# Rates of the conditioning tiles in the first layer: 0.9 a chunk in the query stage, 0.5 in the output projection

## The chip, the cores and the metric

The kernel runs on one core of a Trainium2 chip. The metric is the device time of one execution in microseconds (us), median of the runs. The profile is of one further execution of the same program.

## What is computed

The reference is a trunk of two decoder layers over 256 tokens of 2048 features. Layer 0 mixes tokens by an indexer that keeps 64 keys per query, layer 1 by block attention; a SwiGLU network follows each. Every sub-layer is wrapped in norms and modulated by a conditioning vector c:

```
c_act = silu(c)
for i in range(2):
    mod = c_act @ ada_w[i] + ada_b[i]            # 6 parts of 2048 numbers
    sh1, sc1, g1, sh2, sc2, g2 = split(mod, 6)
    h = rms_norm(x, norm_g[i, 0]) * (1 + sc1) + sh1
    y = (dsa_mixer if i % 2 == 0 else moba_mixer)(h, ...)      # projections, attention, y = o @ w_o
    x = x + g1 * rms_norm(y, norm_g[i, 1])
    h = rms_norm(x, norm_g[i, 2]) * (1 + sc2) + sh2
    x = x + g2 * rms_norm(swiglu(h, ...), norm_g[i, 3])
```

All is in float32. The weights `ada_w` are 2 x 2048 x 12288 numbers, of which each is used once: they are a matrix-vector product that has only to be streamed.

## The kernel before, in words

A weight matrix is read in chunks of 128 partitions x 1024 numbers (512 KB): `load_split` (line 247) issues the load into a `raw` buffer (5 of them), then ScalarE (ACT) copies it to `hi`, a rounded float32r part, and VectorE (DVE) writes the rest, `lo = raw - hi` (line 245; 4 buffers each). TensorE (PE) multiplies by both. All loads are issued by SyncE (SP, "SPq" in the profile), one after the other in program order: an issue that must wait for its buffer holds all later ones up.

The conditioning weights come as tiles of 128 x 2048 (1 MB) into the two `ada` buffers. A column tile (`ada_tile`, line 148) is multiplied with c on VectorE (line 151). A row tile (`ada_row_tile`, line 163) is multiplied on TensorE (line 171); after the 16th, ScalarE copies the sum out (line 176). A buffer is free for the next tile once its product is done.

When a tile is issued is set by a table of rates. `pace` fills a queue of tiles and sets `Pace.rate`; after each chunk load `tick` (line 202) adds the rate to `Pace.due` and issues one tile for each whole number reached. Here the queue holds 48 tiles: parts 4 and 3 of layer 0 (32 column tiles), mixed with 16 row tiles. `Pace.due` starts at 5.0 and three tiles go first. The order that comes of it on each engine is written by a scheduler that follows the program's order, priorities and its own estimate of the durations.

Two stages use this queue. In the query stage (lines 888 to 896) there are four head groups; each loads 8 chunks of `a_in`, multiplies them (lines 309 to 312), copies the sum out (line 340), rotates it (`rope_heads`, lines 657 to 663) and attends (`attend`: scores on lines 678 and 684, softmax on 692 to 699, transposes and the second product on 708 to 717). In the output projection (`out_proj`, line 898) there are four column groups g of 8 chunks of `a_o`, multiplied on lines 369 and 374. After each of the first three the tail reads the sums (`Tail.one`: lines 486 to 491, on ScalarE and VectorE). Before the fourth, `ahead` issues four chunks of `f_in` for the network that follows and holds the ticks, so that only 24 of the 32 chunks tick. The next stage (`cross`) ends the tail and starts the network; it needs all 48 tiles.

Of the kernel before, what the change touches and what calls it, by code (L numbers as in the profile page):

```python
# [50 lines left out]
def trunk(ctx, tc, xT, xn, c, c_cols, pos, consts, mod_b, gains, ada, ada_rows, a_small, a_in, a_o, b_in, b_o, f_in, f_out, out):  # L51
# [145 lines left out]
    def pace(parts, rate):  # L197
        assert not Pace.queue, len(Pace.queue)
        Pace.queue = [(ada_tile, layer_, p, j) for layer_, p in parts for j in range(KT)]
        Pace.rate, Pace.due = rate, 0.0  # L200
# [23 lines left out]
    def gate_cols(layer, part, norm):  # L224
        out = sm.tile([P, KT], F32, tag="cols", name="cols", bufs=8)
        V.tensor_add(out, cols(modraw, layer, part, 6), cols(modb, layer, part, 6))
        V.tensor_mul(out, out, cols(gain, layer, norm, 4))
        return out
# [491 lines left out]
    def ffn_groups(layer, which):  # L720
        return lambda hs: [TokenGroup([f_in[layer, n, i] for i in range(KT // 2)], 2, hs) for n in which]
# [101 lines left out]


    Pace.ahead = True
    pace([(0, 4), (0, 3)], 1.1)
    rows = [(ada_row_tile, 0, 2, k) for k in range(KT)]
    Pace.queue = [t for i in range(4) for t in Pace.queue[2 * i:2 * i + 2] + rows[4 * i:4 * i + 4]] + Pace.queue[8:]
    Pace.due = 5.0
# [68 lines left out]
    def out_proj(w, o_t, tail, groups):  # L898
        for g in range(4):
            if g == 3:  # L900
                first = ahead(groups)
            grp = TokenGroup([w[g, i] for i in range(8)], 2, lambda k: o_t[k // 2][:, k % 2, :]).run(APART if g == 3 else 0)
            if g < 3:
                tail.take(g, grp)
        return tail, grp, None, first

    Pace.ahead = False
    Pace.rate = 0.3
    end = out_proj(a_o, o_t, Tail(gate_cols(0, 2, 1), x2), ffn_groups(0, (0, 1)))
    h, first, x2 = cross(*end, scale_cols(0, 4, 2), shift_cols(0, 3), True)  # L910
    pace([(0, 5), (1, 1), (1, 0), (1, 2)], 0.36)
# [112 lines left out]
```

## Time and profile before

| | |
|---|---|
| runs | 2355.26, 2356.88, 2359.01 us; median 2356.88 |
| profiled execution | 2359.11 us, of which the span from first to last instruction is 2357.3 |
| busy shares of the span | PE 96%, DVE 68%, ACT 48% |
| mean granted clock of TensorE | 0.979 |
| DMA | 609.26 MB, mean 258 GB/s |

The spans of the stages are read from the chain of waits: the query stage ends when the last head group's sums are copied out, at 362 us, and the output projection runs from 366 to 462 us. Times within the trace are from the start of the span. "PEclk" is the share of TensorE's full clock that was granted. A wait is named by the line that waited and the one that let it go.

### The profile page before, as it was taken

What the parts mean: (1) busy time and instruction counts of PE and PEld (TensorE: products, weight loads), DVE (VectorE), ACT (ScalarE), POOL (GpSimd) and SP (SyncE); (2) the same over time, 40 slices, a digit from 0 to 9 for tenths busy, and PEclk for the clock granted to TensorE, in tenths of its full rate; (3) what the DMA queues carried; (4) which work ended last, traced back from release to release, by engine and by line L of the source; (5) the groups of instructions that cost most, each with busy time, mean ns of one, the idle gap of its engine ahead of it and who ended that gap; (6) DMA issues with size and microseconds to landing.
All of it is one profiled execution on the core that took longest, in us unless ns stands there. A gap on an engine that the chain in (4) does not pass through costs nothing.

```text
span 2357.3 us, 29222 instructions
## 1 busy us (share of the span) xinstructions
PE 2256.1 (96%) x10908; PEld 1874.3 (80%) x10908; DVE 1610.2 (68%) x2248; ACT 1123.1 (48%) x1675; POOL 0.4 (0%) x5
## 2 busy tenths in 40 slices
PE   5779889999999999999999999999999999999998
PEld 4667677778888888888878888887888888888886
DVE  7968588667777777755677888566665556554555
ACT  3334455564444444444556666555444444434443
POOL 0000000000000000000000000000000000000000
PEclk7889999999999999999999999999999999999999
DMA  9887888549888888955647898573667776655563
GB/s 385 320 338 283 325 315 326 181 171 355 324 335 328 324 329 323 329 189 190 212 141 297 322 347 294 175 231 121 228 237 236 243 241 226 209 192 191 190 208 126
DMA packets 145296, 609.26 MB, mean 258 GB/s; under 512 B 16449, under 2 KB 17153, under 8 KB 124417
## 3 DMA queue, kind: packets, MB, share of 16 engines
q1 hardware_dynamic: 145154, 607.41, 72.9%
q8 instruction: 85, 1.39, 0.2%
q14 instruction: 57, 0.47, 0.1%
HBM read 605.08 MB, written 2.13 MB: 258 GB/s over the span
## 4 chain that ended last, share of the span: by engine, by line
PE 87%; DVE 6%; DMA 3%; ACT 3%; issue 1%; SPq 0%; DVEq 0%; ACTq 0%
PE acc L369 47%; PE acc L374 23%; PE acc L304 5%; PE acc L316 3%; DVE blk L158 2%; PE acc L309 1%; PE acc L310 1%; DVE lo L245 1%; DMA raw<-a_in 1%; PE acc L312 1%; DMA blk<-ada 1%; PE bank L736 1%; ACT hi L245 1%; PE acc L171 1%; PE bank L714 1%
## 5 line engine op out<-in xcount | busy, mean ns | idle before, releaser
L245 DVE TENSOR_TENSOR lo<-raw,hi 128x1024 fp32r<-128x1024 f32 x736 | 895.0, 1223 | 564.7 <-ACT hi L245 557.1
L369 PE MATMUL acc<-hi,blk 128*128 128x512 f32 x4928 | 1242.9, 392 | 13.0 <-ACT blk L245 7.3
L245 ACT ACTIVATE hi<-raw 128x1024 fp32r<-128x1024 f32 x736 | 775.0, 1059 | 928.8 <-PE acc L369 769.2
L369 PEld LDWEIGHTS acc<-hi,blk 128*128 128x128 f32 x4928 | 921.5, 188 | 205.3 <-ACT blk L245 8.1
L374 PE MATMUL acc<-lo,blk 128*128 128x512 f32 x2464 | 671.2, 390 | 0.0
L374 PEld LDWEIGHTS acc<-lo,blk 128*128 128x128 f32 x2464 | 463.8, 188 | 97.6
L151 DVE SCALAR_TENSOR_TENSOR ada<-ada,c_b 128x2048 f32<-128x2048 f32 x144 | 329.2, 2286 | 37.1 <-DMA ada<-ada 36.3
L309 PE MATMUL acc<-blk,hi 128*128 128x256 f32 (+1 forms) x400 | 114.4, 315 | 44.1 <-ACT hi L245 42.4
L304 PE MATMUL acc<-blk,hi 128*128 128x512 f32 x512 | 136.9, 396 | 0.0
L310 PE MATMUL acc<-blk,hi 128*128 128x256 f32 (+1 forms) x400 | 112.9, 312 | 18.0 <-DVE blk L245 18.0
L309 PEld LDWEIGHTS acc<-blk,hi 128*128 128x128 f32 (+1 forms) x400 | 85.9, 216 | 51.0 <-ACT hi L245 46.5
L310 PEld LDWEIGHTS acc<-blk,hi 128*128 128x128 f32 (+1 forms) x400 | 86.4, 217 | 21.5 <-DVE blk L245 18.7
L304 PEld LDWEIGHTS acc<-blk,hi 128*128 128x128 f32 x512 | 90.1, 189 | 13.8
L316 PEld LDWEIGHTS acc<-blk,lo 128*128 128x128 f32 x512 | 74.0, 190 | 7.6 <-DVE lo L245 0.5
L158 DVE SCALAR_TENSOR_TENSOR blk<-blk,c_b 128x1024 f32<-128x1024 f32 x64 | 76.5, 1221 | 4.0 <-DMA blk<-ada 3.8
L316 PE MATMUL acc<-blk,lo 128*128 128x256 f32 x512 | 77.6, 283 | 0.1
L312 PE MATMUL acc<-blk,lo 128*128 128x256 f32 (+1 forms) x400 | 64.6, 299 | 2.7 <-DVE lo L245 2.6
L312 PEld LDWEIGHTS acc<-blk,lo 128*128 128x128 f32 (+1 forms) x400 | 56.5, 202 | 10.5 <-issue 5.5
L245 ACT ACTIVATE blk<-bank 128x512 fp32r<-128x512 f32 (+1 forms) x76 | 38.3, 507 | 25.3 <-PE bank L715 13.5
L245 DVE TENSOR_TENSOR blk<-bank,blk 128x512 fp32r<-128x512 f32 (+1 forms) x76 | 43.3, 574 | 7.6 <-ACT blk L245 7.4
L584 ACT ACTIVATE t<-bank,cols 128x128 f32<-128x128 f32 x48 | 20.3, 452 | 50.1 <-DVE t L583 50.1
L729 DVE TENSOR_TENSOR t<-acc,t 128x256 f32<-128x256 f32 x88 | 33.6, 417 | 3.2 <-ACT t L728 3.2
(202 smaller groups left out, 1148.2 us busy)
## 6 DMA issues: line engine op xcount, KB each, us to landing
raw<-f_in SPq DMA_DIRECT2D x352, 512.0 KB, 4.3
ada<-ada SPq DMA_DIRECT2D x144, 1024.0 KB, 6.6
raw<-f_out SPq DMA_DIRECT2D x176, 512.0 KB, 4.3
raw<-b_in SPq DMA_DIRECT2D x96, 512.0 KB, 5.8
blk<-ada SPq DMA_DIRECT2D x64, 512.0 KB, 10.2
raw<-a_in SPq DMA_DIRECT2D x64, 512.0 KB, 7.3
ada<-ada_rows SPq DMA_DIRECT2D x16, 1024.0 KB, 6.9
raw<-a_o SPq DMA_DIRECT2D x32, 512.0 KB, 5.4
```

Of the source, the lines that this page charges most:

```text
L151: V.scalar_tensor_tensor(w, w, 1.0, c_b, op0=ALU.mult, op1=ALU.mult, accum_out=modraw[:, mod_col(layer, part, j)])
L158: V.scalar_tensor_tensor(w, w, 1.0, c_b[:, i * (D // 2):(i + 1) * (D // 2)], op0=ALU.mult, op1=ALU.mult, accum_out=sums[:, mod_col(0, part ...
L171: T.matmul(b[32 * q:32 * q + 32, :], c_col[:, k:k + 1].to_broadcast([P, 32]), w[:, 512 * q:512 * q + 512], start=k == 0, stop=k == KT - 1, ...
L245: return A.activation(dst_hi, src, AF.Copy), V.tensor_sub(dst_lo, src, dst_hi)
L304: T.matmul(a[:w, :], w_hi, h, start=k == 0, stop=k == self.nk - 1)
L309: T.matmul(a, w_hi, h[:, :S], start=first, stop=False, skip_group_check=True)
L310: T.matmul(a, w_hi, h[:, S:], start=False, stop=False, skip_group_check=True)
L312: T.matmul(a, w_lo, h[:, :S], start=False, stop=k == self.nk - 1, skip_group_check=True)
L316: T.matmul(a[:w, S:], w_lo, h[:, :S], start=False, stop=False)
L369: T.matmul(self.accs[t], h[:, c + t * P:c + (t + 1) * P], hi[:, r, :], start=k == 0 and c == 0, stop=False)
L374: end = T.matmul(self.accs[t], self.hs(k)[:, t * P:(t + 1) * P], lo[:, r, :], start=False, stop=k == self.nk - 1)
L729: V.tensor_mul(ut, grp.accs[t][:, :256], gt)
```

## The change

Two numbers in the table of rates. With 1.1, the 32 chunk loads of the query stage bring 5 + 35.2 = 40 tiles beside the first three, so 43 of 48 are issued there and 5 are left for the output projection, one each 3 to 4 chunks. With 0.9 they bring 5 + 28.8 = 33, so 36 are issued, and the 12 that are left come one each second chunk: 24 ticks of 0.5 and the 0.8 left over make 12.8. Both times the queue is empty before the next `pace`. The number of loads and of products is the same.

```diff
     Pace.ahead = True
-    pace([(0, 4), (0, 3)], 1.1)
+    pace([(0, 4), (0, 3)], 0.9)
     rows = [(ada_row_tile, 0, 2, k) for k in range(KT)]
...
     Pace.ahead = False
-    Pace.rate = 0.3
+    Pace.rate = 0.5
     end = out_proj(a_o, o_t, Tail(gate_cols(0, 2, 1), x2), ffn_groups(0, (0, 1)))
```

The orders of all engines are the same up to the second head group's middle. On SyncE, from the 13th chunk of the query stage on, before (`raw` is the chunk's buffer, `ada` a tile's; row tiles come from `ada_rows`, column tiles from `ada`; L250, L150 and L166 are their loads):

```order
L166 DMA ada_2178<-ada_rows 128x2048
L150 DMA ada_2184<-ada 128x2048
L150 DMA ada_2217<-ada 128x2048
L250 DMA raw_2280<-a_in 128x1024
L166 DMA ada_2250<-ada_rows 128x2048
L166 DMA ada_2286<-ada_rows 128x2048
L250 DMA raw_2316<-a_in 128x1024
L166 DMA ada_2322<-ada_rows 128x2048
L250 DMA raw_2352<-a_in 128x1024
```

The same place with the change:

```order
L166 DMA ada_2238<-ada_rows 128x2048
L250 DMA raw_2268<-a_in 128x1024
L150 DMA ada_2274<-ada 128x2048
L250 DMA raw_2301<-a_in 128x1024
L150 DMA ada_2307<-ada 128x2048
L250 DMA raw_2334<-a_in 128x1024
L166 DMA ada_2340<-ada_rows 128x2048
L250 DMA raw_2370<-a_in 128x1024
L166 DMA ada_2376<-ada_rows 128x2048
```

The 13th chunk is issued ahead of two tiles that it followed, the 14th ahead of three, and so on. From the 13th to the 32nd chunk 24 tiles stand among the 20 chunks before, and 17 with the change.

On SyncE in the output projection, about its second column group, before:

```order
L150 DMA ada_3581<-ada 128x2048
L250 DMA raw_3596<-a_o 128x1024
L250 DMA raw_3614<-a_o 128x1024
L250 DMA raw_3632<-a_o 128x1024
L150 DMA ada_3638<-ada 128x2048
L250 DMA raw_3667<-a_o 128x1024
L250 DMA raw_3687<-a_o 128x1024
L250 DMA raw_3705<-a_o 128x1024
```

The same place with the change:

```order
L150 DMA ada_3569<-ada 128x2048
L250 DMA raw_3584<-a_o 128x1024
L250 DMA raw_3602<-a_o 128x1024
L150 DMA ada_3608<-ada 128x2048
L250 DMA raw_3623<-a_o 128x1024
L250 DMA raw_3655<-a_o 128x1024
L150 DMA ada_3661<-ada 128x2048
L250 DMA raw_3678<-a_o 128x1024
```

A tile now stands before each pair of chunks up to the 24th chunk; before, the fifth and last stood before the 17th.

On ScalarE at the end of the third column group, before (`raw_3795` and `hi_3797` are its last chunk, `raw_3852` and `hi_3854` the first chunk of the fourth group; `ada_3832`, `ada_3837`, `blk_3842` and `blk_3848` take the chunks of `f_in`; L486 reads the third group's sums):

```order
L245 ACTIVATE ada_3837<-raw_3835 128x1024
L245 ACTIVATE hi_3797<-raw_3795 128x1024
L245 ACTIVATE hi_3854<-raw_3852 128x1024
L245 ACTIVATE hi_3874<-raw_3872 128x1024
L245 ACTIVATE hi_3892<-raw_3890 128x1024
L245 ACTIVATE hi_3910<-raw_3908 128x1024
L486 ACTIVATE t2_3813,st_3327<-acc_3673 128x512
L245 ACTIVATE blk_3842<-raw_3840 128x1024
L491 ACTIVATE t2_3818,st_3327<-blk_3482 128x512
L486 ACTIVATE t2_3820,st_3327<-acc_3674 128x512
```

The same place with the change:

```order
L245 ACTIVATE hi_3797<-raw_3795 128x1024
L245 ACTIVATE ada_3832<-raw_3830 128x1024
L245 ACTIVATE ada_3837<-raw_3835 128x1024
L486 ACTIVATE t2_3813,st_3306<-acc_3664 128x512
L245 ACTIVATE blk_3842<-raw_3840 128x1024
L491 ACTIVATE t2_3818,st_3306<-blk_3467 128x512
L486 ACTIVATE t2_3820,st_3306<-acc_3665 128x512
L245 ACTIVATE blk_3848<-raw_3846 128x1024
L245 ACTIVATE hi_3854<-raw_3852 128x1024
L245 ACTIVATE hi_3874<-raw_3872 128x1024
```

Before, four chunks of the fourth group are converted ahead of the instruction that waits for the third group's end; with the change none is, and five instructions stand between that wait's end and the first of them. VectorE has the same shift with its `lo` parts.

## Rows read from the trace of the kernel before

**Rows 1.** Busy time by stretch, clock, DMA; the first line names the columns

```profile
core 0: us, PE busy (x) PEld busy (x) DVE busy (x) ACT busy (x) POOL busy (x), PEclk, DMA share, GB/s
244.00:366.00 122.00, 97.41 (x659) 85.85 (x651) 85.03 (x139) 60.00 (x140) 0.00 (x0) 0.92 0.88 329
391.00:411.00 20.00, 20.00 (x90) 16.57 (x89) 16.27 (x18) 10.15 (x16) 0.00 (x0) 1.00 0.98 382
391.00:462.00 71.00, 71.00 (x315) 58.81 (x314) 50.35 (x78) 36.03 (x55) 0.00 (x0) 1.00 0.76 267
450.00:480.00 30.00, 28.26 (x123) 21.00 (x122) 18.56 (x69) 13.53 (x27) 0.00 (x0) 1.00 0.21 69
```

**Rows 2.** Chain of waits: start us, us, what

```profile
319.52 0.66 ACT blk L340 x2
...
362.12 0.66 ACT blk L340 x2
...
391.29 1.82 PE acc L369 x8
...
394.01 1.81 PE acc L369 x8
...
461.56 0.47 PE acc L374 x2
```

**Rows 3.** Waits of PE, 244 to 366 us: total us, times, longest

```profile
PE acc L309 <- ACT hi L245: 16.9, 10, 4.4
```

**Rows 4.** Waits of ACT in the same stretch

```profile
ACT hi L245 <- DMA raw<-a_in: 31.7, 8, 7.3
```

**Rows 5.** Waits of SP's queue, 244 to 356 us

```profile
SPq L150 <- DVE ada L151: 26.7, 8, 4.4
```

**Rows 6.** SP's issues in order of time: start us, us

```profile
244.66 2.94 SPq L150 DMA_DIRECT2D ada<-ada  x2
...
350.71 0.38 SPq L250 DMA_DIRECT2D raw<-a_in  x1
```

**Rows 7.** DMA, 244.5 to 351 us: issues, KB each, us to landing

```profile
DMA packets 6100, 34.47 MB, mean 324 GB/s; under 512 B 686, under 2 KB 686, under 8 KB 3110
...
ada<-ada SPq DMA_DIRECT2D x20, 1024.0 KB, 5.6
raw<-a_in SPq DMA_DIRECT2D x20, 512.0 KB, 6.7
ada<-ada_rows SPq DMA_DIRECT2D x4, 1024.0 KB, 6.4
```

**Rows 8.** DVE by line, 391 to 447 us: busy us, mean ns, idle before

```profile
L245 DVE TENSOR_TENSOR lo<-raw,hi 128x1024 fp32r<-128x1024 f32 x20 | 24.4, 1225 | 13.1 <-ACT hi L245 13.1
L151 DVE SCALAR_TENSOR_TENSOR ada<-ada,c_b 128x2048 f32<-128x2048 f32 x3 | 6.9, 2287 | 0.7 <-DMA ada<-ada 0.7
L489 DVE SCALAR_TENSOR_TENSOR t<-blk,x 128x512 f32<-128x512 f32 x6 | 4.1, 690 | 0.1
L487 DVE TENSOR_TENSOR blk<-acc,blk 128x512 f32<-128x512 f32 x6 | 4.1, 687 | 0.0
```

**Rows 9.** Busy time by stretch, second layer's attention at rate 0.5

```profile
1270.00:1310.00 40.00, 40.00 (x233) 35.24 (x232) 34.36 (x40) 19.74 (x29) 0.00 (x0) 1.00 0.91 361
1350.00:1390.00 40.00, 40.00 (x238) 35.37 (x237) 37.02 (x65) 25.75 (x58) 0.00 (x0) 1.00 0.95 354
```

**Rows 10.** DMA, second layer's attention, 1350 to 1410 us

```profile
ada<-ada SPq DMA_DIRECT2D x10, 1024.0 KB, 7.2
```

**Rows 11.** DMA, 366 to 470 us

```profile
ada<-ada SPq DMA_DIRECT2D x4, 1024.0 KB, 10.3
```

**Rows 12.** ACT in order of time, end of the third column group

```profile
440.50 0.58 ACT L486 ACTIVATE t<-acc 128x512 f32<-128x512 f32 x1
...
444.64 2.00 ACT L245 ACTIVATE hi<-raw 128x1024 fp32r<-128x1024 f32 x2
```

**Rows 13.** PE in order of time, start of the output projection

```profile
366.20 3.01 PE L369 MATMUL acc<-hi,blk 128*128 128x512 f32 x8 [3.16 <-ACT hi L245]
```

## The prediction

> **What bounds the kernel now.** The change touches two stages, so I read the busy time by stretch first [rows 1]. From 244 to 366 us, the last three head groups of the query stage, TensorE is busy 97.4 of 122 us, its granted clock is 0.92 (a mean of stretches at 2.4 GHz and some at 1.2), and the DMA engines are busy 88% at 329 GB/s. From 391 to 462 us, the output projection, TensorE is busy all of 71 us at clock 1.00 while DMA stands at 76%, and from 450 us on it falls to 21%. So one stage has too much to load and the next has room.
>
> Then the waits, to see that the first stage really lacks data. TensorE waits 16.9 us in ten pieces for ScalarE's `hi` conversion [rows 3], and this conversion waits 31.7 us in eight pieces for the chunk itself [rows 4]. One step further back, SP's issues of column tiles wait 26.7 us for VectorE to finish the product that frees a tile buffer [rows 5]. SP issues in order, so a chunk that stands behind such a tile is issued late by the same time. A tile takes 5.6 us from issue to landing [rows 7] and 2.29 us on VectorE [rows 8], 7.9 us in all, and there are two buffers: about 4 us a tile at best. From the first issue at 244.66 to the last chunk at 350.71 [rows 6] there are 24 tiles and 20 chunks, thus 106.05 / 24 = 4.42 us a tile. Between the ends of two head groups lie 42.6 us (319.52 to 362.12 [rows 2]).
>
> The output projection is bound by TensorE: two chunks 2.72 us apart (391.29 to 394.01 [rows 2]).
>
> **The change part by part.** *Query stage.* Seven tiles leave the 244.66 to 350.71 stretch (24 become 17). A tile is 1024 KB, 1.049 MB, so 7.34 MB go. At that stretch's mean of 324 GB/s [rows 7] they took 22.7 us. The same seven by their own pace, 7 x 4.42, are 30.9 us: this holds if the ring of two tile buffers alone sets the pace and the chunks ride along free. As the other end I take half of the 22.7, 11.3 us: near the end of each head group ScalarE's queue carries the softmax before the next `hi`, and in that half the chunks are not what it waits for. I choose 22.7, because 88% busy DMA is nearer to a limit by bytes than to a limit by the ring. What could become late next is TensorE. It has 24.6 us of idle time in the stretch, and 8% of 122, 9.8 us, are lost to the lower clock, 34.4 us together; 22.7 fits under it. VectorE also loses 7 x 2.29 = 16 us of products there and does not become the bound. Three of the seven tiles go already from ahead of the second head group's last four chunks, so more than a third of the gain should be there before that group ends.
>
> *Output projection, the load.* Twelve tiles instead of five, one with each pair of chunks. A pair with its tile is 2 x 0.524 + 1.049 = 2.10 MB. TensorE needs 2 x 2.72 = 5.44 us for the pair. From 391 to 411 us the DMA engines moved 382 GB/s [rows 1], which makes 5.49 us, 0.05 more. In the second layer's attention, where the same rate of 0.5 is in use and chunks are as large, the two stretches moved 361 and 354 GB/s while TensorE was busy all 40 us [rows 9]; at 361 the pair takes 5.81 us, 0.37 more. Over 12 pairs this is 0.6 to 4.4 us. The start has some lead to eat, so I take 1 us. VectorE: two `lo` at 1.225, a tile at 2.287, and the tail's L487 and L489, 8.2 us over three column groups or 0.68 us a pair [rows 8], are 5.42 of 5.44 us. That leaves nothing over, but in the second layer it was busy 37.0 of 40 us [rows 9] and TensorE did not wait.
>
> One rule of the Trainium skill speaks against this part: the page "SBUF — State Buffer", section "Summary: rules for kernel authors", says to reckon some 358 GB/s for transfers from HBM, not the higher rate of the fabric. By it a pair would take an estimated 5.86 us and the 12 pairs would cost 5.0 us in place of 1, which would make 2345 us of the forecast below, within its range. The trace does not agree for 20 us on end, with 382 GB/s [rows 1], so I keep the smaller cost.
>
> *Output projection, the order.* This is the part that I expect to cost most. With the change, the first `hi` of the fourth column group stands on ScalarE behind the L486 that waits for the third group's end, and five instructions behind it. Before, four such conversions were already done. In the trace that row of instructions is there as it will be: L486 starts at 440.50 and the next pair of `hi` at 444.64, each of the pair 1.00 us [rows 12]. So a `hi` is ready 4.14 + 1.00 = 5.14 us after L486 starts. L486 can start when the first of the two sums is whole, two matmuls or 0.47 us [rows 2] before TensorE runs out. TensorE then waits 4.7 us, which it did not before. After a wait of 3.16 us the eight matmuls of the next chunk took 3.01 us [rows 13] instead of 1.81 [rows 2], as the clock was down (the mean of 244 to 366 us is 0.92 for such reasons); this adds 1.2. Together 5.9 us. At least 3 us, if the transfers let ScalarE run ahead of this reckoning; at most 8, if `lo`, which has six instructions ahead of it on VectorE, is later still.
>
> All 48 tiles are now done by the 24th chunk; eight chunks, 21.8 us, remain until `cross` needs them, so no wait for them is charged. What follows is the same work in the same order, only earlier.
>
> Sum: -22.7 + 1 + 5.9 = -15.8 us. The profiled execution took 2359.11 us, 2.2 more than the median of the runs, 2356.88. So 2343.3 on its scale, and 2341 us beside the median. I call under 0.2%, 4.7 us, no change that a measurement could tell.
>
> **The rivals.**
>
> *The ring sets the pace.* If the tile buffers, not the bytes, bound the query stage, the gain is 30.9 and the result 2356.9 - 30.9 + 6.9 = 2333 us. For it: the 26.7 us of SP's waits for the products. Against it: DMA at 88%.
>
> *ScalarE's queue sets half of the query stage.* Then 11.3 us are gained and 6.9 paid, -4.4, which makes 2352 or 2353 us. For it: of the 24.6 us of TensorE's idle time only 16.9 are waits for `hi`, and these conversions stand among softmax instructions. Against it: the eight waits for a chunk, 31.7 us, are as long as three quarters of a head group.
>
> *The two stages together are bound by bytes.* The same 48 tiles and 64 chunks must be in before the projection ends; if that set its end, moving tiles would do nothing: 2357. Against it: the DMA engines fall to 69 GB/s from 450 us on [rows 1]. So the change does what it says only if the later stage has that room, and it seems to.
>
> *Slower: the ring moves to the output projection.* There a tile is followed by two chunks and its landing counts: from 366 to 470 us the four tiles took 10.3 us to land [rows 11]. With 2.29 us of product and two buffers, a tile each 6.3 us, 0.86 more than TensorE's 5.44, 10 us over twelve. At a landing of 12 us it is 7.15 us a tile, 1.7 more, 20.5 us; with the 5.9 of the order this is 26.4 against 22.7 gained: 2357 + 3.7, some 2361 us, and each further microsecond of landing costs 6 more. It decides from 7 - 5.44 = 1.4 us too much a tile on, that is, a landing of about 11.4 us. For it: the 10.3, and VectorE at 5.42 of 5.44 us, where each wait for a tile holds up the `lo` behind it. Against it: those four were issued behind up to four chunks at once; at rate 0.5 in the second layer tiles took 7.2 us to land [rows 10].
>
> **How the numbers follow.** I give my forecast (a gain of 8 to 21 us) 0.47, the ring in the query stage 0.20, ScalarE's queue 0.15, bound by bytes 0.06, slower 0.12. The third splits into 0.06 faster, 0.07 same and 0.02 slower. So faster is 0.47 + 0.20 + 0.06 = 0.73, same 0.06 + 0.07 = 0.13, slower 0.12 + 0.02 = 0.14. The forecast's own range is 2336 to 2349. For eight in ten I go down to 2328 (the ring with a cheap projection, -30.9 + 3) and up to 2357 (half of the gain with the dear ends of both costs, -11.3 + 8 + 4.4).
>
> **What the profile would show.** The last chunk of the query stage issued near 328 instead of 350.7 and the last head group's L340 near 340; the waits of `hi` for a chunk well under 31.7 us; a new wait of TensorE of 4 to 5 us at the start of the fourth column group, and no other over 1 us in the projection; DMA over 90% there for the first 24 chunks. I am wrong if the head groups still take 42 us each, if TensorE starves for chunks in the projection, or if the fourth group starts without a wait.

## The result and the profile after

The changed kernel takes 2340.15 us in the median (2337.88 to 2341.61, 4 runs) against 2357.95 for the kernel before in the same runs: a ratio of 0.993 with a 95% interval of 0.9917 to 0.9944, 13 to 20 us faster. The forecast was 2341. The profiled execution took 2338.76 us, its span 2337.0, at a mean granted clock of 0.984.

Times within two traces can only be subtracted from a common mark. SyncE's order is the same in both kernels past a pair of chunks that was issued at 211.62 us before and at 208.41 after; 3.2 us of the difference of the profiled executions thus arose ahead of the change and say nothing of it. From this mark I read two distances: to the first L340 of the last head group (the query stage), and from there to the first matmul of `cross`, L369, which reads the `ada` buffers that hold the first chunks of `f_in` (the projection). SP's issues, the mark before and then after:

```profile
211.62 1.71 SPq L250 DMA_DIRECT2D raw<-a_in  x2
...
208.41 0.86 SPq L250 DMA_DIRECT2D raw<-a_in  x2
```

The chain of waits before (start us, us, what), with the end of the second head group and the start of `cross`:

```profile
277.94 0.66 ACT blk L340 x2
...
465.57 1.42 PE acc L369 x5
```

| | mark | last L340 | `cross` | query stage | projection |
|---|---|---|---|---|---|
| before | 211.62 | 362.12 | 465.57 | 150.5 | 103.45 |
| after | 208.41 | 333.05 | 445.15 | 124.6 (-25.9) | 112.1 (+8.65) |

Sum -17.2 us, beside -17.8 of the medians. Each distance is from one profile. A second profile of the order before (the first experiment) reads 147.65 for the query stage, 2.85 less than the 150.5 here, so -25.9 stands for something between -23 and -26.

The chain of waits of the kernel after has the end of the second head group, that of the fourth, which answers to the 362.12 of [rows 2], and the start of `cross`:

```profile
262.30 0.66 ACT blk L340 x2
...
333.05 0.66 ACT blk L340 x2
...
445.15 1.43 PE acc L369 x5
```

Before, the second head group ended at 277.94, counted from the mark 12.4 us later than now. Nearly half of the 25.9 us is gained before the last two head groups, where three of the seven tiles are missing. Between the last two groups' ends lie 34.6 us now (298.42 to 333.05), 42.6 before.

SP's issues, as [rows 6]: the 13th chunk of the query stage and the 32nd, the last.

```profile
238.93 0.33 SPq L250 DMA_DIRECT2D raw<-a_in  x1
...
319.32 0.38 SPq L250 DMA_DIRECT2D raw<-a_in  x1
```

The DMA between them, as [rows 7]:

```profile
DMA packets 4965, 27.04 MB, mean 334 GB/s; under 512 B 554, under 2 KB 554, under 8 KB 2782
...
ada<-ada SPq DMA_DIRECT2D x13, 1024.0 KB, 6.9
raw<-a_in SPq DMA_DIRECT2D x20, 512.0 KB, 7.3
ada<-ada_rows SPq DMA_DIRECT2D x4, 1024.0 KB, 4.8
```

It holds 17 tiles and 20 chunks as counted from the order, and lasts 80.4 us; before, 24 tiles and 20 chunks took 106.05. By what is issued these are 28.3 MB at 352 GB/s against 35.65 MB at 336. The stage is shorter mainly because it carries less, and a little because it carries it faster.

The waits of ACT, 244 to 350 us, as [rows 4]: 31.7 us in eight pieces have become 11.2 in five.

```profile
ACT hi L245 <- DMA raw<-a_in: 11.2, 5, 4.9
```

The waits of PE, 228 to 450 us. The second row answers to [rows 3]: 4.6 us where there were 16.9. The first row holds the new wait in the projection, 4.3 (4.35 in the order of time below), and 1.12 and 0.74 us at its beginning, where there were 3.16 [rows 13]. Of the third row, 2.1 us also stand there: `attend` of the last head group waits for its rotated input.

```profile
PE acc L369 <- ACT hi L245: 6.2, 3, 4.3
PE acc L309 <- ACT hi L245: 4.6, 6, 1.5
PE bank L678 <- ACT blk L663: 3.1, 2, 2.1
...
PE acc L374 <- DVE lo L245: 0.5, 1, 0.5
```

Busy time by stretch, columns as in [rows 1]. The first row is the query stage with the same 659 matmuls as the 122 us of [rows 1]; both end just before the first matmul of the projection.

```profile
241.00:335.40 94.40, 86.90 (x659) 77.16 (x651) 68.15 (x121) 57.84 (x136) 0.00 (x0) 1.00 0.90 343
350.00:411.00 61.00, 60.28 (x272) 49.29 (x273) 54.98 (x60) 32.44 (x52) 0.00 (x0) 1.00 0.91 353
371.00:391.00 20.00, 20.00 (x90) 16.59 (x89) 15.95 (x17) 8.45 (x11) 0.00 (x0) 1.00 1.02 416
391.00:411.00 20.00, 19.44 (x84) 15.44 (x84) 19.93 (x24) 10.37 (x15) 0.00 (x0) 1.00 0.87 332
411.00:440.00 29.00, 24.65 (x99) 19.88 (x98) 18.71 (x36) 13.82 (x22) 0.00 (x0) 0.88 0.73 236
430.00:460.00 30.00, 27.87 (x122) 20.69 (x120) 18.78 (x70) 13.87 (x27) 0.00 (x0) 1.00 0.16 47
```

In the query stage TensorE now idles 7.5 of 94.4 us and is busy 86.9; before, it idled 24.6 of 122 and was busy 97.4. Of the 27.6 us by which this stretch is shorter, 17.1 are thus idle time, and 10.5 are matmuls that run at a granted clock of 1.00, where it was 0.92. In the projection DMA is 91% busy from 350 to 411 us and TensorE idles 0.7 of these 61; the late room that DMA had is used. Two places in this stage have become dearer. Early in the third column group, while VectorE still works on the second group's sums, it is full (19.93 of 20 us) and TensorE waits 0.47 us for `lo`, with two chunk spacings of 3.48 and 3.09 us instead of 2.72, 1.1 us in all. At the start of the fourth group stands the wait that the order foretold. PE in order of time; the first row is the wait for `lo`, the others the end of the third group and the next two chunks:

```profile
395.08 1.20 PE L374 MATMUL acc<-lo,blk 128*128 128x512 f32 x4 [0.47 <-DVE lo L245]
...
411.93 1.07 PE L374 MATMUL acc<-lo,blk 128*128 128x512 f32 x4
417.34 3.78 PE L369 MATMUL acc<-hi,blk 128*128 128x512 f32 x8 [4.35 <-ACT hi L245]
420.92 1.65 PE L374 MATMUL acc<-lo,blk 128*128 128x512 f32 x4
422.41 2.01 PE L369 MATMUL acc<-hi,blk 128*128 128x512 f32 x8
```

ACT at that place, as [rows 12]: from the start of L486 to the pair of `hi` are 3.66 us, where 4.14 were read.

```profile
412.58 0.60 ACT L486 ACTIVATE t<-acc 128x512 f32<-128x512 f32 x1 [2.73 <-PE acc L374]
...
416.24 2.00 ACT L245 ACTIVATE hi<-raw 128x1024 fp32r<-128x1024 f32 x2
```

The load of the fourth group's first chunk also comes late. SP's issue of it, before and then after:

```profile
428.18 0.33 SPq L250 DMA_DIRECT2D raw<-a_o  x1
...
410.13 0.33 SPq L250 DMA_DIRECT2D raw<-a_o  x1
```

Before, this is 12.3 us ahead of the L486 that ends the third group (440.50 [rows 12]); now it is 2.5 us ahead (412.58). The last semaphore update of its landing is at 413.56 in the trace. A `hi` that ScalarE had begun right then would have ended at some 414.6. TensorE ran dry at 412.99, so by this estimate 1.6 of the 4.35 us would have been left whatever ScalarE's order, and 2.7 come from the order alone.

### The profile page after: what moved, and what is told of

It is laid out like the page before. It is cut to its first block, busy times and chain, and to the rows that moved or that the text cites. A ratio compares the mean times of both kernels' runs of the same rounds, so it can differ in the third digit from the quotient of the medians.

```text
span 2337.0 us, 29216 instructions
## 1 busy us (share of the span) xinstructions
PE 2245.6 (96%) x10908; PEld 1865.0 (80%) x10908; DVE 1608.8 (69%) x2248; ACT 1122.6 (48%) x1675; POOL 0.4 (0%) x5
## 4 chain that ended last, share of the span: by engine, by line
PE 85%; DVE 7%; ACT 4%; DMA 3%; issue 1%; SPq 0%; DVEq 0%; ACTq 0%
PE acc L369 47%; PE acc L374 23%; PE acc L304 5%; PE acc L316 3%; DVE blk L158 2%; DVE lo L245 1%; ACT hi L245 1%; PE acc L312 1%; PE acc L310 1%; PE acc L309 1%; PE bank L736 1%; DMA blk<-ada 1%; DMA raw<-a_in 1%; PE bank L714 1%; DMA ada<-ada_rows 1%
## 5 line engine op out<-in xcount | busy, mean ns | idle before, releaser
L369 PE MATMUL acc<-hi,blk 128*128 128x512 f32 x4928 | 1244.3, 393 | 16.2 <-ACT blk L245 7.3
L369 PEld LDWEIGHTS acc<-hi,blk 128*128 128x128 f32 x4928 | 922.5, 189 | 208.6 <-ACT blk L245 8.1
L309 PE MATMUL acc<-blk,hi 128*128 128x256 f32 (+1 forms) x400 | 106.7, 300 | 31.8 <-ACT hi L245 30.1
L310 PE MATMUL acc<-blk,hi 128*128 128x256 f32 (+1 forms) x400 | 105.9, 298 | 17.3 <-DVE blk L245 17.3
L309 PEld LDWEIGHTS acc<-blk,hi 128*128 128x128 f32 (+1 forms) x400 | 79.9, 201 | 38.6 <-ACT hi L245 32.5
L310 PEld LDWEIGHTS acc<-blk,hi 128*128 128x128 f32 (+1 forms) x400 | 80.6, 203 | 20.7 <-DVE blk L245 18.0
```

Source lines behind the costliest of these rows:

```text
L309: T.matmul(a, w_hi, h[:, :S], start=first, stop=False, skip_group_check=True)
L310: T.matmul(a, w_hi, h[:, S:], start=False, stop=False, skip_group_check=True)
L369: T.matmul(self.accs[t], h[:, c + t * P:c + (t + 1) * P], hi[:, r, :], start=k == 0 and c == 0, stop=False)
```

## The experiments

The rates below are those of the query stage and of the projection; the changed kernel has 0.9 and 0.5. Ratios are to the kernel before in the same runs.

**The second number alone.** The theory says that nothing is gained in the projection itself: its rate only takes up what the query stage gives away.

```diff
-    Pace.rate = 0.3
+    Pace.rate = 0.5
```

(with the query stage at 1.1, as before.)

> Rates 1.1 and 0.5: the second number alone. 43 tiles still go in the query stage, and the five left come one each second chunk. Theory (the gain comes from seven tiles leaving the query stage, and part of it is paid at the start of the fourth column group): the last head group's sums are copied out at 359 to 363 us as before, the fourth group starts without a wait because its first conversions stand ahead again, and the time is that of before, 2355 to 2360 us. Rival (the rate in the projection is worth something by itself, for instance by a denser use of the transfers): 5 us or more below before.

Measured: 2356.03 us against 2356.49, ratio 0.9997 (0.9988 to 1.0005). The waits of PE from 366 us, behind the projection's first wait, to 480 us hold no `hi` at all; the row that is left belongs to `cross`:

```profile
PE acc L369 <- ACT blk L245: 3.4, 2, 2.5
```

With few tiles left the queue is empty early, and the chunks of the fourth group run ahead again. What the change gains comes from the query stage alone, and the wait at the fourth group comes from the later tiles, not from the number 0.5.

SyncE's order in the query stage is that of the kernel before, so this run reads the old stage a second time: from the mark at 211.66 to the last head group's L340 at 359.31 are 147.65 us, where the first profile has 150.5. Differences of 3 us between single profiles of this stage say nothing.

**The wait taken away.** `out_proj` calls `ahead`, which issues four chunks of `f_in`, before the fourth column group. In this kernel the first layer issues them behind that group's first two chunks. The loads and all rates are those of the changed kernel.

```diff
-            if g == 3:
+            if g == 3 and layer:
                 first = ahead(groups)
...
+            wait = [lambda: late.append(ahead(groups))] if g == 3 and not layer else []
+            late = []
-            grp = TokenGroup([w[g, i] for i in range(8)], 2, lambda k: o_t[k // 2][:, k % 2, :]).run(APART if g == 3 else 0)
+            grp = TokenGroup([w[g, i] for i in range(8)], 2, lambda k: o_t[k // 2][:, k % 2, :]).run(APART if g == 3 else 0, wait)
...
```

(`layer` is a new argument of `out_proj`, 0 in the first layer; `run` calls what waits behind the second chunk.)

> The changed kernel with one thing moved: in layer 0 the four chunks for the next network are issued behind the fourth column group's first two chunks, not ahead of them, so that two conversions of the fourth group stand ahead of the instruction that waits for the third group's end. Theory (the wait of 4.35 us and the slow chunk behind it, 2.5 us, come from the order on ScalarE alone): TensorE starts the fourth group without a wait of over 1 us, perhaps waits 1 to 2 us at its third chunk, and the time is 3 to 7 us under the changed kernel, 2333 to 2337 us. Rival (VectorE or the transfers set the projection's end, and the wait only shows it): the wait moves to another place in the fourth group and the time stays within 2 us of 2340.

Measured: 2333.04 us, ratio 0.9899 (0.9885 to 0.9912), some 7 us less than the changed kernel; by the two distances the query stage is 124.25 us, as after, and the projection 107.25 instead of 112.1. PE in order of time shows the fourth group's second chunk (its last matmuls), which follows the first without a pause, and what is left of the wait at the third:

```profile
416.99 1.07 PE L374 MATMUL acc<-lo,blk 128*128 128x512 f32 x4
419.48 2.11 PE L369 MATMUL acc<-hi,blk 128*128 128x512 f32 x8 [1.42 <-ACT hi L245]
```

So the wait of 4.35 us goes when the group's first two chunks stand ahead of `f_in`, and with the slow chunk behind it, it cost about what was charged for it: 4.85 us are back and 1.4 are still paid. That the place in ScalarE's queue alone was the cause isn't shown: the edit moves the loads as well as their conversions, and in the changed kernel the first chunk landed too late for some 1.6 us of the wait. This version beats both kernels.

**Three chunks first.** As above, with `f_in` behind the third chunk.

```diff
-            grp = TokenGroup([w[g, i] for i in range(8)], 2, lambda k: o_t[k // 2][:, k % 2, :]).run(APART if g == 3 else 0, wait)
+            grp = TokenGroup([w[g, i] for i in range(8)], 2, lambda k: o_t[k // 2][:, k % 2, :]).run(APART if g == 3 else 0, wait, 2)
...
```

(the new third argument is the chunk after which `run` calls what waits; it was always the second.)

> Rates 0.9 and 0.5 with the four chunks for the next network behind the fourth group's first three chunks instead of two. Theory: the wait of 1.42 us that was left at the third chunk goes or becomes smaller, 2331 to 2334 us against 2333.0 with two. Rival (the conversions for the next network come so late that the next stage waits): over 2335 us.

Measured: 2334.38 us, ratio 0.9913 (0.9897 to 0.9929), no better than two. The waits of PE from 337 to 470 us show that the 1.42 us are gone:

```profile
PE acc L369 <- ACT hi L245: 1.9, 2, 1.1
```

The projection is 106.4 us against 107.25 with two, a gain of 0.9, less than these runs resolve. The expectation of a further gain was not borne out.

**More tiles in the projection's first half.** Rates 0.9 and 0.75: the same query stage, but the 12 tiles come within 16 chunks, so the last half of the stage is free of them.

```diff
-    Pace.rate = 0.5
+    Pace.rate = 0.75
```

> Rates 0.9 and 0.75: the same 36 and 12 tiles, but the twelve come within the first 16 chunks of the projection. Theory: the query stage ends as in the changed kernel (last sums copied out at 331 to 335 us); the fourth group starts without a wait, as its conversions stand ahead again (6.9 us back); but a tile each 1.33 chunks is 1.75 MB in 3.63 us of TensorE, 482 GB/s, more than the 416 that the changed kernel's best 20 us show, so the projection's first half starves by 12 x (1.75/0.40 - 3.63) = 9 us less its lead. Together 2336 to 2344 us. Rival (the transfers have room left): 2333 us.

Measured: 2342.2 us, ratio 0.9941 (0.9928 to 0.9953). PE, 360 to 400 us, in order of time: there is no wait at the fourth group, but four in the first half of the projection.

```profile
376.12 3.58 PE L369 MATMUL acc<-hi,blk 128*128 128x512 f32 x8 [2.09 <-ACT hi L245]
...
384.66 2.11 PE L369 MATMUL acc<-hi,blk 128*128 128x512 f32 x8 [1.18 <-ACT hi L245]
...
393.58 2.12 PE L369 MATMUL acc<-hi,blk 128*128 128x512 f32 x8 [0.47 <-ACT hi L245]
...
398.24 2.11 PE L369 MATMUL acc<-hi,blk 128*128 128x512 f32 x8 [1.64 <-ACT hi L245]
```

These are 5.4 us, and the 2.09 again stands ahead of a slow chunk; the projection takes 113.4 us against 112.1. Here the load itself makes TensorE wait: three tiles and four chunks, 5.24 MB, in 10.88 us want 482 GB/s, and DMA moved 362 from 375 to 405 us, as the busy time by stretch (columns as above) has it:

```profile
375.00:405.00 30.00, 25.59 (x102) 19.99 (x103) 27.60 (x30) 13.70 (x20) 0.00 (x0) 0.94 0.94 362
```

At 0.5 the same sum is 386, and TensorE hardly waited. The wait at the fourth group can be traded for this one; nothing is won.

**Fewer and more tiles moved.** Rates 1.0 and 0.4 move 3 tiles instead of 7, rates 0.8 and 0.65 move 10.

```diff
-    pace([(0, 4), (0, 3)], 0.9)
+    pace([(0, 4), (0, 3)], 1.0)
...
-    Pace.rate = 0.5
+    Pace.rate = 0.4
```

> Rates 1.0 and 0.4: three tiles leave the query stage instead of seven, eight come in the projection. Theory (each tile that leaves the query stage gives back its share of the transfers, 25.7/7 = 3.7 us by the changed kernel's trace): last sums copied out some 11 us earlier than before, near 351; one conversion of the fourth group stands ahead of the instruction that waits, so the wait there is 1 to 3 us; together 2346 to 2350 us. Rival (the gain is one step that comes whole with the first tiles moved, for instance the two tiles ahead of the 13th chunk): 2338 to 2342 us.

Measured: 2343.84 us, ratio 0.9955 (0.9939 to 0.9971), 2 us below the theory's range and about as far above the rival's. The query stage is 136.3 us, 14.2 less than before for three tiles (11.4 against the second profile of the old order). The projection, 102.0 us, is not longer than before, and the waits of PE from 350 to 480 us hold only the old one at its start, in the second row:

```profile
PE acc L369 <- ACT blk L245: 3.4, 2, 2.5
PE acc L369 <- ACT hi L245: 3.2, 1, 3.2
```

```diff
-    pace([(0, 4), (0, 3)], 0.9)
+    pace([(0, 4), (0, 3)], 0.8)
...
-    Pace.rate = 0.5
+    Pace.rate = 0.65
```

> Rates 0.8 and 0.65: ten tiles leave the query stage, fifteen come in the projection. Theory: in the query stage 10 x 3.7 = 37 us at most, less where TensorE and the chain through ScalarE become the bound, so 28 to 34; in the projection 0.65 tile and a chunk are 1.21 MB in 2.72 us, 443 GB/s, over the 416 seen, 24 chunks with 15 tiles 28.3 MB at 400 GB/s 71 us against 65, so 6 us are paid beside the 6.9 of the fourth group's start: 2336 to 2343 us, no better than the changed kernel by more than 4 us. Rival (the query stage goes on gaining in proportion and the projection has room): 2328 to 2331 us.

Measured: 2337.12 us, ratio 0.9931 (0.9912 to 0.9951), the same as the changed kernel. The query stage is 120.5 us, -30.0 for ten tiles; the projection 110.9. PE in order of time, where it waits from 360 us on:

```profile
369.00 2.12 PE L369 MATMUL acc<-hi,blk 128*128 128x512 f32 x8 [2.18 <-ACT hi L245]
...
386.90 2.12 PE L369 MATMUL acc<-hi,blk 128*128 128x512 f32 x8 [1.27 <-ACT hi L245]
...
413.64 3.41 PE L369 MATMUL acc<-hi,blk 128*128 128x512 f32 x8 [4.35 <-ACT hi L245]
```

The three rates together give the gain of the query stage as 14.2, 25.9 and 30.0 us for 3, 7 and 10 tiles; against the second profile of the old order it is 11.4, 23.0 and 27.2. The first tiles brought 3.8 to 4.7 us each, the next four 2.9, the last three 1.4. The first step's excess is within what two profiles differ; the last step's fall is not, for the four profiles at 0.9 lie between 124.25 and 124.9 us, and the two at 0.8 at 120.5 and 121.4. The stretch with the same matmuls shows why it falls, as the first row by stretch of the kernel after; here the second profile of the order before, then 3 and 10 tiles moved (the last with two matmuls fewer):

```profile
244.00:363.30 119.30, 95.92 (x659) 84.16 (x651) 84.98 (x139) 60.08 (x140) 0.00 (x0) 0.93 0.90 337
...
243.80:351.60 107.80, 91.45 (x659) 79.11 (x651) 78.50 (x133) 60.03 (x140) 0.00 (x0) 0.98 0.91 341
...
241.50:330.70 89.20, 87.82 (x657) 76.79 (x656) 64.69 (x117) 57.81 (x135) 0.00 (x0) 1.00 0.87 330
```

TensorE's idle time falls from 23.4 or 24.6 us to 16.4, 7.5 and 1.4, 2 to 2.7 us for each tile up to the last. Its busy time falls by 9.0 to 10.5 us up to seven tiles, while the granted clock comes back to 1.00, and no further. With ten tiles moved TensorE itself bounds the stage, with 1.4 us of idle time in 89.

**Both together.** Rates 0.8 and 0.65 with `f_in` behind two chunks of the fourth group (the edits are those above).

> Rates 0.8 and 0.65 with the four chunks for the next network behind the fourth group's first two. Theory (the order's cost and the load's cost are separate and add): 5 to 7 us under the run with 0.8 and 0.65 alone, 2330 to 2337 us. Rival (once transfers bound the projection, the wait at the fourth group is only where the late transfers show, and moving it gives nothing): within 2 us of that run.

Measured: 2331.63 us, ratio 0.9903 (0.9888 to 0.9918). Against the same rates without it, the move of `f_in` is worth 5.5 us by the medians and 2.8 by the projection's distance (110.9 to 108.1). PE, from 400 us on:

```profile
404.23 2.12 PE L369 MATMUL acc<-hi,blk 128*128 128x512 f32 x8 [0.80 <-ACT hi L245]
...
419.57 2.14 PE L369 MATMUL acc<-hi,blk 128*128 128x512 f32 x8 [1.42 <-ACT hi L245]
```

It isn't told apart from the version with 0.9 and 0.5. The best that these runs found is thus about 2332 us, 1% below the kernel before.

**Bytes or the ring.** The kernel before, with the product of the column tiles of parts 3 and 4 over a quarter of their 2048 columns; the rest of the sum is left out. The loads stay whole. A product is then 1.6 us shorter, and so is the time in which it holds one of the two tile buffers.

```diff
-        V.scalar_tensor_tensor(w, w, 1.0, c_b, op0=ALU.mult, op1=ALU.mult,
+        n = D // 4 if layer == 0 and part in (3, 4) else D
+        V.scalar_tensor_tensor(w[:, :n], w[:, :n], 1.0, c_b[:, :n], op0=ALU.mult, op1=ALU.mult,
```

> The kernel before, in which the product of a column tile of parts 3 and 4 of layer 0 covers 512 of its 2048 columns (the rest of the sum is left out); the tile is loaded whole. The bytes are the same, a product is some 0.6 us instead of 2.29. Theory A (bytes set the query stage's pace): its last chunk is issued at 346 to 351 us as before, and DMA stays near 324 to 340 GB/s. Theory B (the ring of two tile buffers, landing plus product, sets it): a tile buffer is free 1.7 us sooner, 0.86 us a tile over 21 to 24 tiles, so the last chunk is issued 15 to 20 us earlier, at 330 to 335, and DMA runs at 370 GB/s or more there. VectorE's relief may add a few us in either case.

Measured: 2351.91 us, ratio 0.9977 (0.9967 to 0.9987); the last chunk of the query stage was issued at 341.55 us, between the two theories and nearer the one by bytes. VectorE from 240 to 350 us, and the DMA from 235 to 350 us:

```profile
L152 DVE SCALAR_TENSOR_TENSOR ada<-ada,c_b 128x512 f32<-128x512 f32 x20 | 13.8, 688 | 9.9 <-DMA ada<-ada 9.8
```

```profile
DMA packets 7128, 40.14 MB, mean 349 GB/s; under 512 B 783, under 2 KB 783, under 8 KB 3684
...
ada<-ada SPq DMA_DIRECT2D x22, 1024.0 KB, 6.9
```

The product fell from 2.29 to 0.69 us, and the tile's landing was 6.9 us instead of 5.6 [rows 7]; in the second profile of the old order it is 6.1. So of the 1.6 us that a buffer came free earlier, 0.8 to 1.3 were spent on a longer transfer. From the 13th to the 32nd chunk it took 94.6 us with 21 tiles; in the order before 103.0 and, in the second profile, 101.3, with 22. Less the one tile, at 4.4 to 4.7 us, the shorter product gave 2 to 4 us. By the ring alone, 1.6 us less for each tile over two buffers, it would have given 0.8 x 21 = 17. So the product has a small part in the pace; that the rest is the transfers' follows from this and from the gain per tile moved, and no run changes the bytes of a tile alone.

## Why the prediction was right, point by point

- **Query stage**, -22.7 forecast, -25.9 measured, or -23.0 against the second profile of the old order. That moving tiles out of this stage gains the time is shown by three rates; that a tile is priced by its bytes is what fits best: by the full ring, the rival, it would have been 30.9. The price of 3.24 us a tile held on the average of seven (3.3 to 3.7), and not beyond, as TensorE had little idle time left by then (7.5 us of 24.6). The recovered clock, which the prediction counted as room, is 10.5 us of the gain. The first part of the gain was where it was said to be. The last chunk was forecast near 328 and stands at 319.32, the last L340 near 340 and stands at 333.05; 322.5 and 336.3 without the 3.2 us that arose earlier.
- **Projection, the load**, +1 forecast. Of the 8.65 us that the stage is longer, 4.35 are the wait and 2.5 the slow chunk; 1.1 stand early in the third column group, where VectorE was full as forecast, and 0.7 belong to its start, where waits of 1.12, 2.1 and 0.74 us have taken the place of one of 3.16 and its slow chunk. So 1.1 to 1.8, within the 0.6 to 4.4, but a pair's loads were mis-sized and their lead over TensorE hid it: from the 8th chunk of `a_o` to the 24th (the two rows of SP's issues below) SP took 50.8 us, 6.35 a pair and not 5.49 to 5.81, and two `blk<-row_d` loads of 512 KB that stand among them were not in the sum. From a chunk's issue to the moment when TensorE is ready for it were 11.5 us at the stage's start (324.08 to 335.57) and 2.9 at the fourth group (410.13 to 412.99). That no other wait would be over 1 us held but for the start, and DMA was 91% busy from 350 to 411 us as forecast. By the rule of the Trainium skill ("SBUF — State Buffer", "Summary: rules for kernel authors") an estimated 5 us would have been lost; the 61 us from 350 to 411 ran at 353 GB/s, near the rule's 358, but with 416 in 20 of them, and TensorE idled only 0.7 us.

```profile
349.35 2.37 SPq L250 DMA_DIRECT2D raw<-a_o  x2
...
400.15 0.38 SPq L250 DMA_DIRECT2D raw<-a_o  x1
```

- **Projection, the order**, +5.9 forecast, 6.85 measured. The wait of 4.7 was 4.35 and stands at the place and on the `hi` that the order named, and ScalarE's row of instructions is what it ended with. But the prediction took for granted that the chunk had landed by then; the lead of its load was almost gone, and by the landing at 413.56 some 1.6 us of the wait belong to the load. The slow chunk was forecast with 1.2 and cost 2.5: from 417.34 to the next chunk at 422.57 in the chain of waits are 5.23 us instead of 2.72. The term was mis-sized: I counted the eight matmuls with `hi` and not the four with `lo` behind them, though the row that follows [rows 13] in the trace before has them slow too (1.81 us, with 1.07 at full clock):

```profile
369.01 1.81 PE L374 MATMUL acc<-lo,blk 128*128 128x512 f32 x4
```

- **The sum**, -15.8 forecast, -17.2 by the distances and -17.8 by the medians. The closeness is in part luck: costs 1.8 us larger than charged stand against a gain that was 0.3 to 3.2 us larger, and each of these is within the 3 us that single profiles differ.
- **The rivals.** Half of the query stage by ScalarE's queue (2352) fell with the 23 to 26; bound by bytes over both stages (2357) fell with the late room that was used, from 69 GB/s [rows 1] to 47 at 430 to 460 us while the end came earlier. The ring moved to the projection (2361) needed a landing of 11.4 us there (the 7 - 5.44 = 1.4 of its working should be 6.84 - 5.44; the 11.4 is right); it was 7.6, by the DMA from 350 to 411 us:

```profile
ada<-ada SPq DMA_DIRECT2D x8, 1024.0 KB, 7.6
```

- **Not settled:** how the bytes and the small share of the ring divide the price of a tile, and how ScalarE's order and the late load divide the wait at the fourth group, beyond the estimate of 2.7 and 1.6 us. No run moves one of the two alone.

## What to carry to other kernels

Where two stages share a stream that only has to be in by the end of the second, put it where the engine that bounds the stage has slack on the DMA: read the DMA share and the operand waits of each stage, price a moved tile by its bytes at the stage's rate, and expect the price to fall once TensorE has hardly any idle time left and its clock is back. In the stage that takes the tiles, follow the lead of the loads over TensorE: as long as it lasts, it hides a price that was set too low. Then read the order of the engine that prepares the operands: a load that is issued later can put its conversion behind an instruction that waits for the group's end, and a wait of 4 us cost 7 here with the slow chunk behind it. Issuing the next group's first two chunks ahead of what is not yet needed gave more than any further tuning of the rates.

## What was not expected of the hardware

- The DMA engines moved 416 GB/s for 20 us at a busy share of 1.02, more than in any stretch that was read before the change (382).
- A tile's landing time is not a constant of the transfer: in the query stage its median was 5.6 and 6.1 us in two profiles of the old order, and 6.9 with seven tiles moved as with a shorter product. What the ring of two buffers would give, worked out from one such landing time (17 us for the shorter product), came out at 2 to 4 us.
- After the wait of 4.35 us the twelve matmuls of a chunk took 5.23 us instead of 2.72, and the granted clock of the stretch from 411 to 440 us is 0.88, a mean over 2.4 GHz and the lower of its two levels, while it is 1.00 in all the other stretches of this kernel that are shown.
